# Tiles for the first pair's sums of weights, and the order of units in the head

## The chip, the cores and the metric

The kernel runs on one core of a Trainium2 chip. TensorE (PE) multiplies, ScalarE (ACT) and VectorE (DVE) work elementwise, GpSimd (POOL) takes a few elementwise operations, and SyncE (SP) issues the transfers from HBM. Each engine works through its own instructions in the order in which they stand. The metric is the device time of one execution in microseconds (us).

## What is computed

Two decoder layers work on 512 tokens of width 1024. Each layer is a feed-forward, a token mixer and a second feed-forward. The feed-forwards are what the change touches:

```python
D_MODEL, SEQ, DEPTH, D_FF = 1024, 512, 2, 2816

def swiglu(h, w_up, w_down):
    gate, up = jnp.split(h @ w_up, 2, axis=-1)
    return (jax.nn.silu(gate) * up) @ w_down

for l in range(DEPTH):
    mod = (jnp.einsum('bd,de->be', jax.nn.silu(c), w_ada[l]) + b_ada[l]).reshape(b, 9, d)
    h = modulate(rmsnorm(x, norm_g[l, 0]), mod[:, 0], mod[:, 1])
    x = x + 0.5 * mod[:, 2][:, None] * swiglu(h, w_ffn_in[l, 0], w_ffn_out[l, 0])
    ...          # rmsnorm, modulate, token_mixer, x += mod[:, 5] * y
    h = modulate(rmsnorm(x, norm_g[l, 2]), mod[:, 6], mod[:, 7])
    x = x + 0.5 * mod[:, 8][:, None] * swiglu(h, w_ffn_in[l, 1], w_ffn_out[l, 1])
```

## The kernel before

There are six sub-layers, n = 1 to 6. Numbers 1, 3, 4 and 6 are feed-forwards; 2 and 5 are mixers. In the profiled execution n=3 runs from about 909 to 1268 us, n=4 from there to 1630, and n=6 from about 2158 to the end.

**Products in two parts.** Each float32 operand is split into a rounded high part and the rest. ACT copies the high part (L226 makes `wh` of a weight, L268 `sh`, `ah` of activations) and DVE subtracts it (L230 makes `wl`, L269 `sl`, `al`). Every product is then three matmuls on PE: high by high, low by high, high by low (L274, L276, L278, or the three of L592).

**A feed-forward.** Its 22 blocks of hidden units begin with plain units (two in n=3, 4 and 6, four in n=1), of a gate and an up matrix each. In n=3, 4 and 6 the first three of these four products are the "head" (`head`, L711): 512 tokens in two halves of 256 columns (`HALF`), because the normalised input `h` of the second half comes later. The fourth product ("the fourth unit") follows with all 512 columns. Then come pairs: a pair takes two hidden blocks with seven products in the place of eight (`pair`, `product`, L577 to L648), in the order p = 1, 2, 6, 7, 5, 3, 4, with the next pair's p=1 between 5 and 3. Each of the seven is 24 matmuls of 128x256.

**What a pair needs.** p = 1, 2 and 4 read `h` itself. p = 6, 7, 5 and 3 read four sums of quarters of `h` (`hq`, made in place by `sums`, L559 to L562, and split by `summed` into `sh` and `sl`). On the side of the weights p = 1, 2 and 3 read blocks 11, 21, 22 as they are, and `block` (L233) makes the other four: t1 = w12 - w11 (L246, for p=5), t2 = w22 - t1 (L248, for p=6), w12 = w22 - w12 in place (L250, p=7), w21 = w21 - t2 in place (L253, p=4).

**Rings.** Tiles come from rings of fixed size: raw weights `wraw` 5, `whi` 3, `wlo` 3, the ring of activations `t4k` 10 (sums split, SwiGLU results), and `z` 4. A tile's slot is free once the last reader of its former tile is through. t1 and t2 come from `z` by `z4k`; the four quarters `hq` lie there too and go when `summed` has read them.

**What sets the order.** The program is written sequentially and a scheduler orders the instructions of each engine by their place in the text, the data, the slots of the rings and its own estimate of times. `load` fetches weights in the order of `plan`, two ahead of their use (`AHEAD`), and a pair's sums are made in `load` at p = 6, 7 and 4. The norm of the next half of the tokens (sum of squares L481, the sum over partitions on PE L322, reciprocal root L295 to L307, `h` in L500 to L509) runs on DVE and ACT beside the head.

Of the kernel before, what the change touches and what calls it, by code (L numbers as in the profile page):

```python
# [13 lines left out]
F32 = mybir.dt.float32  # L14
# [6 lines left out]
P = 128  # L21
T = 512
D = 1024
KD = 8
# [10 lines left out]
HALF = (slice(0, 256), slice(256, 512))  # L35
# [38 lines left out]
class Trunk:  # L74
# [44 lines left out]
    def z4k(self, s):  # L119
        t = self.ap_.tile([P, 2 * (T + TAPS - 1)], F32, tag="z", name=self.name(s), bufs=4)  # L120
        return t[:, 0:D]

    def bank(self, tag):
        return self.pp.tile([P, T], F32, tag=tag, name=self.name(tag),
                            bufs={"mm": 4, "s": 3, "o": 1}[tag])
# [76 lines left out]
    def load(self):  # L202
        key = next(self.keys, None)
        if key is None:
            return
        kind = key[0]
        if kind == "up":
            raw, n = self.block(*key[1:]), 1024
        else:
            src, n = self.source(key)  # L210
            raw = self.raw()
            r = raw[:, :n]
            if len(src.shape) == 3:
                r = r.rearrange("p (a b) -> p a b", b=src.shape[2])
            self.nc.sync.dma_start(r, src)
        self.loaded.append((key, *self.halves(key, raw, n)))
# [13 lines left out]
        eng.tensor_tensor(lo[:, :n], raw[:, :n], hi[:, :n].bitcast(F32), op=ALU.subtract)  # L230
        return hi, lo

    def block(self, l, f, j, p):  # L233


        sub = self.nc.vector.tensor_tensor
        if p == 1:
            self.pairs[j] = {}
            for q in (11, 21, 12, 22):
                t = self.raw()  # L240
                self.nc.sync.dma_start(t, self.io["w_up"][l, f, j, (11, 21, 12, 22).index(q)])
                self.pairs[j][q] = t
        b = self.pairs[j]
        if p == 6:
            b["t1"] = self.z4k("t")
            sub(b["t1"], b[12], b[11], op=ALU.subtract)  # L246
            b["t2"] = self.z4k("t")
            sub(b["t2"], b[22], b["t1"], op=ALU.subtract)  # L248
        elif p == 7:
            sub(b[12], b[22], b[12], op=ALU.subtract)  # L250
        elif p == 4:

            sub(b[21], b[21], b["t2"], op=ALU.subtract)  # L253
        return b[{1: 11, 2: 21, 6: "t2", 7: 12, 5: "t1", 3: 22, 4: 21}[p]]
# [326 lines left out]
    def product(self, l, f, j, p, bank, first):  # L581

        nc = self.nc
        w = self.weight("up", l, f, j, p)
        acts = self.operand(p)
        for mi in range(2):
            o = bank[:, mi * 256:mi * 256 + 256]
            for k in range(4):
                c = slice((mi * 4 + k) * P, (mi * 4 + k + 1) * P)
                for x, (a, b) in enumerate(((0, 0), (1, 0), (0, 1))):  # L590

                    nc.tensor.matmul(o, w[a][:, c], acts[k][b], start=first and (mi, k, x) == (0, 0, 0),  # L592
                                     stop=(k, x) == (3, 2), skip_group_check=True)
# [122 lines left out]
    def head(self, take):  # L716

        ws = [take(j) for j in range(3)]
        ps = [self.bank("mm") for _ in ws]
        for k in range(KD):  # L720
            for j in range(3):
                self.mm(ps[j], ws[j], slice(k * P, (k + 1) * P), self.h[k], k == 0, k == KD - 1, HALF[0])
        for j in range(3):
            self.mmk(ps[j], ws[j], self.h, range(KD), 0, KD - 1, HALF[1])
        return ps
# [531 lines left out]
```

## Time and profile before

| | us |
|---|---|
| median of three runs | 2522.96 (2520.47 to 2523.03) |
| the profiled execution | 2520.49 |
| its span | 2518.7 |
| PE busy | 2470.0 (98%) |
| PE weight load busy | 2186.7 (87%) |
| DVE busy | 1924.0 (76%) |
| ACT busy | 1179.6 (47%) |

The span is what the trace covers; 1.8 us lie around it. A row of a timeline gives start, busy time of one and, in brackets, the idle time of the engine before it with what ended it. [...] Matmuls overlap in the pipeline, so the time of a run of them is told by start to start and not by the busy time of one.

### The profile page before, as it was taken

What the parts mean: (1) busy time and instruction counts of PE and PEld (TensorE: products, weight loads), DVE (VectorE), ACT (ScalarE), POOL (GpSimd) and SP (SyncE); (2) the same over time, 40 slices, a digit from 0 to 9 for tenths busy, and PEclk for the clock granted to TensorE, in tenths of its full rate; (3) what the DMA queues carried; (4) which work ended last, traced back from release to release, by engine and by line L of the source; (5) the groups of instructions that cost most, each with busy time, mean ns of one, the idle gap of its engine ahead of it and who ended that gap; (6) DMA issues with size and microseconds to landing.
All of it is one profiled execution on the core that took longest, in us unless ns stands there. A gap on an engine that the chain in (4) does not pass through costs nothing.

```text
span 2518.7 us, 37996 instructions
## 1 busy us (share of the span) xinstructions
PE 2470.0 (98%) x15072; PEld 2186.7 (87%) x15072; DVE 1924.0 (76%) x3344; ACT 1179.6 (47%) x1941; POOL 15.3 (1%) x25
## 2 busy tenths in 40 slices
PE   7999999999999999999989999999999999999999
PEld 6889898888778889898989898898887888898988
DVE  8989876999855478888688796669997654885855
ACT  6535243665653355353455353436665433553523
POOL 0000000000000000000000000000000000000000
PEclk9999999999999999999999999999999999999999
DMA  8565644322223224646325554322222233133332
GB/s 275 185 238 171 231 148 130 95 63 68 78 85 109 94 67 133 234 134 234 126 67 159 209 172 130 101 81 79 64 80 67 82 111 100 59 106 96 111 98 86
DMA packets 97748, 312.21 MB, mean 124 GB/s; under 512 B 10345, under 2 KB 17257, under 8 KB 97570
## 3 DMA queue, kind: packets, MB, share of 16 engines
q1 hardware_dynamic: 97424, 309.65, 38.3%
q8 instruction: 118, 1.93, 0.3%
q14 instruction: 60, 0.49, 0.1%
q10 hardware_dynamic: 146, 0.14, 0.0%
HBM read 307.62 MB, written 6.06 MB: 125 GB/s over the span
## 4 chain that ended last, share of the span: by engine, by line
PE 86%; DVE 9%; ACT 3%; issue 2%; DMA 1%; SPq 0%; DVEq 0%; ACTq 0%
PE mm L592 16%; PE mm L274 14%; PE mm L276 14%; PE mm L278 14%; PE s L592 12%; PE mm L845 3%; PE mm L843 3%; PE mm L841 3%; PE s L904 2%; DVE wl L230 2%; PE o L973 1%; PE s L946 1%; DVE wr L778 1%; ACT wh L226 1%; ACT hh L502 1%
## 5 line engine op out<-in xcount | busy, mean ns | idle before, releaser
L226 ACT ACTIVATE wh<-wr 128x1024 fp32r<-128x1024 f32 (+1 forms) x481 | 485.5, 1011 | 601.2 <-PE mm L278 295.0
L230 DVE TENSOR_TENSOR wl<-wr,wh 128x1024 fp32r<-128x1024 f32 (+1 forms) x476 | 551.6, 1161 | 215.7 <-ACT wh L226 214.5
L276 PE MATMUL mm<-hh,wl 128*128 128x512 f32 (+1 forms) x776 | 281.2, 366 | 5.2 <-DVE wl L230 5.2
L274 PE MATMUL mm<-hh,wh 128*128 128x512 f32 (+1 forms) x776 | 281.1, 365 | 4.8 <-ACT hh L502 2.9
L278 PE MATMUL mm<-al,wh 128*128 128x512 f32 (+1 forms) x752 | 284.8, 379 | 0.0
L276 PE MATMUL mm<-ah,wl 128*128 128x512 f32 (+1 forms) x752 | 283.9, 378 | 0.0
L274 PE MATMUL mm<-ah,wh 128*128 128x512 f32 (+1 forms) x752 | 283.4, 377 | 0.0
L592 PE MATMUL mm<-sh,wh 128*128 128x256 f32 x936 | 268.4, 287 | 12.8 <-ACT wh L226 10.0
L278 PE MATMUL mm<-hl,wh 128*128 128x512 f32 (+1 forms) x776 | 274.9, 365 | 0.7 <-DVE hl L509 0.6
L592 PE MATMUL mm<-sh,wl 128*128 128x256 f32 x936 | 267.6, 286 | 0.9 <-DVE wl L230 0.9
L592 PE MATMUL mm<-sl,wh 128*128 128x256 f32 x936 | 267.3, 286 | 0.0
L518 DVE SCALAR_TENSOR_TENSOR x<-mm,res,x 128x512 f32<-128x512 f32 (+1 forms) x124 | 86.0, 696 | 144.8 <-PE mm L278 144.6
L592 PEld LDWEIGHTS mm<-sh,wh 128*128 128x128 f32 x936 | 181.7, 194 | 14.9 <-ACT wh L226 11.0
L592 PEld LDWEIGHTS mm<-sh,wl 128*128 128x128 f32 x936 | 182.2, 195 | 1.6 <-DVE wl L230 1.2
L592 PEld LDWEIGHTS mm<-sl,wh 128*128 128x128 f32 x936 | 182.2, 195 | 0.0
L843 PE MATMUL mm<-wl,hh 128*128 128x384 f32 x512 | 179.5, 351 | 0.0
L841 PE MATMUL mm<-wh,hh 128*128 128x384 f32 x512 | 179.4, 350 | 0.0
L845 PE MATMUL mm<-wh,hl 128*128 128x384 f32 x512 | 178.8, 349 | 0.0
L592 PE MATMUL s<-hl,wh 128*128 128x256 f32 x624 | 175.2, 281 | 0.0
L592 PE MATMUL s<-hh,wh 128*128 128x256 f32 x624 | 174.8, 280 | 0.0
L592 PE MATMUL s<-hh,wl 128*128 128x256 f32 x624 | 174.0, 279 | 0.5 <-DVE wl L230 0.5
L440 DVE SCALAR_TENSOR_TENSOR ada<-ada,cb 128x1024 f32<-128x1024 f32 x144 | 172.9, 1215 | 1.2 <-DMA ada<-in_w_ada 1.0
(217 smaller groups left out, 5536.8 us busy)
## 6 DMA issues: line engine op xcount, KB each, us to landing
wr<-in_w_up SPq DMA_DIRECT2D x156, 512.0 KB, 3.7
ada<-in_w_ada SPq DMA_DIRECT2D x144, 512.0 KB, 5.5
wr<-in_w_down SPq DMA_DIRECT2D x64, 512.0 KB, 5.3
wr<-in_w_qkv SPq DMA_DIRECT2D x64, 384.0 KB, 3.2
wr<-in_w_gate SPq DMA_DIRECT2D x48, 512.0 KB, 3.6
wr<-in_w_down SPq DMA_DIRECT2D x32, 384.0 KB, 3.2
wr<-in_w_branch SPq DMA_DIRECT2D x24, 512.0 KB, 3.7
wr<-in_w_u SPq DMA_DIRECT2D x16, 512.0 KB, 3.6
```

Of the source, the lines that this page charges most:

```text
L226: nc.scalar.activation(hi[:, :n], raw[:, :n], AF.Copy)
L230: eng.tensor_tensor(lo[:, :n], raw[:, :n], hi[:, :n].bitcast(F32), op=ALU.subtract)
L274: nc.tensor.matmul(ps[:, rng], w[0][:, wcol], ah[:, rng], start=start, stop=False)
L276: nc.tensor.matmul(ps[:, rng], w[1][:, wcol], ah[:, rng], start=False, stop=False)
L278: nc.tensor.matmul(ps[:, rng], w[0][:, wcol], al[:, rng], start=False, stop=stop)
L440: nc.vector.scalar_tensor_tensor(w, w, 1.0, cb, op0=ALU.mult, op1=ALU.mult, accum_out=self.mod[l][:, e:e + 1])
L518: self.nc.vector.scalar_tensor_tensor(self.x[d][:, rng], ps[:, rng], self.res[l][:, 8 * s + d:8 * s + d + 1], self.x[d][:, rng], op0=ALU.m ...
L592: nc.tensor.matmul(o, w[a][:, c], acts[k][b], start=first and (mi, k, x) == (0, 0, 0), stop=(k, x) == (3, 2), skip_group_check=True)
L841: nc.tensor.matmul(o, hi[:, hs], w[0][:, ws], start=k == 0, stop=False)
L843: nc.tensor.matmul(o, hi[:, hs], w[1][:, ws], start=False, stop=False)
L845: nc.tensor.matmul(o, lo[:, hs], w[0][:, ws], start=False, stop=k == KD - 1)
L904: nc.tensor.matmul(ps[:, 0:w], q[r, a, qs], k[r, b, 0:w], start=x == 0, stop=x == 2)
```

## The change

It has two parts. First, `load` hands `block` the place from which t1 and t2 come: for the first pair of each feed-forward (j = 2 in n=1, j = 1 elsewhere) that is the ring `t4k` by a new `t4w`, for all other pairs `z4k` as before. Second, `head` writes the matmuls of the first half of the tokens as units 0 and 1 together over the eight chunks k, then unit 2, where it wrote all three units per chunk. `head` is used by the mixers too.

```diff
+    def t4w(self, s):
+        return self.t4k([P, D], F32, s)
 ...
         if kind == "up":
-            raw, n = self.block(*key[1:]), 1024
+            early = key[3] == (2 if key[1:3] == (0, 0) else 1)
+            raw, n = self.block(*key[1:], self.t4w if early else self.z4k), 1024
 ...
-    def block(self, l, f, j, p):
+    def block(self, l, f, j, p, home):
 ...
         if p == 6:
-            b["t1"] = self.z4k("t")
+            b["t1"] = home("t")
             sub(b["t1"], b[12], b[11], op=ALU.subtract)
-            b["t2"] = self.z4k("t")
+            b["t2"] = home("t")
             sub(b["t2"], b[22], b["t1"], op=ALU.subtract)
 ...
-        for k in range(KD):
-            for j in range(3):
-                self.mm(ps[j], ws[j], slice(k * P, (k + 1) * P), self.h[k], k == 0, k == KD - 1, HALF[0])
+        for js in ((0, 1), (2,)):
+            for k in range(KD):
+                for j in js:
+                    self.mm(ps[j], ws[j], slice(k * P, (k + 1) * P), self.h[k], k == 0, k == KD - 1, HALF[0])
```

Line numbers after the change are 5 higher from `block` on: L246 becomes L251, L230 becomes L235, L269 becomes L274, L509 becomes L514. The rows of SP and of POOL stand in the same order in both kernels. DVE's change in n=3 at three places, and in n=4 and n=6 in the same way. wr_9092, wr_9094, wr_9096 and wr_9098 are blocks 11, 21, 12 and 22 of the first pair; wl_8925 and wl_8931 are the low parts of the head's third unit and of the fourth unit; wl_9101, 9136, 9171, 9201 and 9236 those of p = 1, 2, 6, 7 and 5; sl_9205, 9240 and 9280 the sums of activations of p = 6, 7 and 5.

DVE in n=3, from the end of the first half's `h` to the norm of the second, before:

```order
L518 SCALAR_TENSOR_TENSOR x<-mm_8664,res_113,x 128x256
L509 SCALAR_TENSOR_TENSOR hl_97<-hx_8784,shift_109,hh_96 128x256
L481 TENSOR_TENSOR ssq<-ssq,sq_8814 128x256
L325 TENSOR_SCALAR ts_8848<-s_8843 128x2
L295 TENSOR_SCALAR rs_8850<-ts_8848 128x2
L298 TENSOR_SCALAR nh_8851<-ts_8848 128x2
L296 TENSOR_SCALAR rs_8850<-rs_8850 128x2
L303 SCALAR_TENSOR_TENSOR rt_8852<-rs_8850,nh_8851 128x1 x2
L307 SCALAR_TENSOR_TENSOR rs_8850<-rt_8852,rs_8850 128x1
L230 TENSOR_TENSOR wl_8925<-wr_8922,wh_8924 128x1024
```

and after:

```order
L523 SCALAR_TENSOR_TENSOR x<-mm_8664,res_113,x 128x256
L514 SCALAR_TENSOR_TENSOR hl_97<-hx_8784,shift_109,hh_96 128x256
L251 TENSOR_TENSOR t_9166<-wr_9096,wr_9092 128x1024
L486 TENSOR_TENSOR ssq<-ssq,sq_8814 128x256
L235 TENSOR_TENSOR wl_8925<-wr_8922,wh_8924 128x1024
L330 TENSOR_SCALAR ts_8848<-s_8843 128x2
L300 TENSOR_SCALAR rs_8850<-ts_8848 128x2
L303 TENSOR_SCALAR nh_8851<-ts_8848 128x2
L301 TENSOR_SCALAR rs_8850<-rs_8850 128x2
L308 SCALAR_TENSOR_TENSOR rt_8852<-rs_8850,nh_8851 128x1 x2
```

t1's subtraction (now L251) has come from behind the head to a place ahead of the sum of squares of the second half, and wl_8925 stands ahead of the reciprocal root and no longer inside it.

DVE in n=3, at the end of the second half's `h` (hl_95 and hl_97 are its last two chunks), before:

```order
L509 SCALAR_TENSOR_TENSOR hl_95<-hx_8903,shift_109,hh_94 128x256
L509 SCALAR_TENSOR_TENSOR hl_97<-hx_8908,shift_109,hh_96 128x256
L559 TENSOR_TENSOR hq_8895<-hq_8874,hq_8895 128x1024
L560 TENSOR_TENSOR hq_8874<-hq_8750,hq_8874 128x1024
L230 TENSOR_TENSOR wl_8931<-wr_8928,wh_8930 128x1024
L561 TENSOR_TENSOR hq_8750<-hq_8895,hq_8750 128x1024
```

and after:

```order
L514 SCALAR_TENSOR_TENSOR hl_95<-hx_8903,shift_109,hh_94 128x256
L253 TENSOR_TENSOR t_9168<-wr_9098,t_9166 128x1024
L514 SCALAR_TENSOR_TENSOR hl_97<-hx_8908,shift_109,hh_96 128x256
L564 TENSOR_TENSOR hq_8895<-hq_8874,hq_8895 128x1024
L255 TENSOR_TENSOR wr_9096<-wr_9098,wr_9096 128x1024
L235 TENSOR_TENSOR wl_8931<-wr_8928,wh_8930 128x1024
L565 TENSOR_TENSOR hq_8874<-hq_8750,hq_8874 128x1024
```

t2 (L253) now stands ahead of the last chunk of `h`, and the new w12 (L255) ahead of the low part of the fourth unit, wl_8931; the second of the sums of quarters (L560, now L565) has gone behind it.

DVE in n=3, the first pair's operands, before:

```order
L663 TENSOR_TENSOR sil_9129<-sil_9129,mm_9104 128x512
L269 TENSOR_TENSOR sl_9205<-hq_8750,sh_9204 128x1024
L269 TENSOR_TENSOR sl_9240<-hq_8874,sh_9239 128x1024
L269 TENSOR_TENSOR al_9089<-sil_9129,ah_9088 128x512
L246 TENSOR_TENSOR t_9166<-wr_9096,wr_9092 128x1024
L269 TENSOR_TENSOR sl_9280<-hq_8895,sh_9279 128x1024
L248 TENSOR_TENSOR t_9168<-wr_9098,t_9166 128x1024
L617 TENSOR_TENSOR c_1521_9163<-c_1521_9163,s_9165 128x512
L250 TENSOR_TENSOR wr_9096<-wr_9098,wr_9096 128x1024
L230 TENSOR_TENSOR wl_9171<-t_9168,wh_9170 128x1024
```

and after:

```order
L668 TENSOR_TENSOR sil_9129<-sil_9129,mm_9104 128x512
L235 TENSOR_TENSOR wl_9136<-wr_9094,wh_9135 128x1024
L274 TENSOR_TENSOR al_9089<-sil_9129,ah_9088 128x512
L235 TENSOR_TENSOR wl_9171<-t_9168,wh_9170 128x1024
L274 TENSOR_TENSOR sl_9205<-hq_8750,sh_9204 128x1024
L235 TENSOR_TENSOR wl_9201<-wr_9096,wh_9200 128x1024
L622 TENSOR_TENSOR c_1521_9163<-c_1521_9163,s_9165 128x512
L274 TENSOR_TENSOR sl_9240<-hq_8874,sh_9239 128x1024
L235 TENSOR_TENSOR wl_9236<-t_9166,wh_9235 128x1024
L274 TENSOR_TENSOR sl_9280<-hq_8895,sh_9279 128x1024
```

The three `sl` no longer stand ahead of the sums of weights: for each product its `wl` and its `sl` follow each other, in the order in which PE asks for them. On ACT `wh_9170` (of t2) and `wh_9200` have moved in the same way ahead of the second and third `sh`.

## Rows read from the trace of the kernel before

**Rows 1.** PE's waits by line and releaser: us in total, times, longest us

```profile
PE mm L592 <- ACT wh L226: 10.0, 5, 2.7
PE s L592 <- ACT wh L226: 5.6, 5, 1.3
PE mm L276 <- DVE wl L230: 5.2, 3, 2.0
```

**Rows 2.** PE timeline, first pairs of n=3, 4, 6: start, us, instruction [idle before]

```profile
943.42 0.28 PE L592 MATMUL s<-hl,wh 128*128 128x256 f32 x1
946.31 0.38 PE L592 MATMUL mm<-sh,wh 128*128 128x256 f32 x1 [2.62 <-ACT wh L226]
948.04 0.39 PE L592 MATMUL s<-sh,wh 128*128 128x256 f32 x1 [1.35 <-ACT wh L226]
...
1306.24 0.38 PE L592 MATMUL mm<-sh,wh 128*128 128x256 f32 x1 [2.72 <-ACT wh L226]
...
2194.80 0.58 PE L592 MATMUL mm<-sh,wh 128*128 128x256 f32 x1 [2.62 <-ACT wh L226]
```

**Rows 3.** Chain that ended last, over the span: start, us, piece (first: n=3)

```profile
955.44 8.59 PE mm L592 x72
...
1316.38 8.59 PE mm L592 x72
...
2204.47 8.59 PE mm L592 x72
```

**Rows 4.** Engines by stretch: us, PE, PEld, DVE, ACT, POOL, PEclk, DMA share, GB/s

```profile
948.40:951.70 3.30, 3.30 (x19) 3.30 (x18) 3.30 (x4) 0.55 (x1) 0.00 (x0) 0.51 0.21 27
...
1279.50:1282.80 3.30, 3.30 (x18) 3.30 (x17) 1.97 (x9) 1.08 (x3) 0.00 (x0) 0.51 0.56 159
```

**Rows 5.** DVE timeline, n=3, ahead of the first pair's p=6

```profile
941.62 1.22 DVE L246 TENSOR_TENSOR t<-wr,wr 128x1024 f32<-128x1024 f32 x1
...
943.89 1.22 DVE L248 TENSOR_TENSOR t<-wr,t 128x1024 f32<-128x1024 f32 x1
...
945.63 1.22 DVE L250 TENSOR_TENSOR wr<-wr,wr 128x1024 f32<-128x1024 f32 x1
```

**Rows 6.** ACT timeline, n=3, the same stretch

```profile
945.20 1.06 ACT L226 ACTIVATE wh<-t 128x1024 fp32r<-128x1024 f32 x1 [2.72 <-DVE t L248]
```

**Rows 7.** DVE timeline, n=3, between the halves of the head

```profile
915.63 0.47 DVE L509 SCALAR_TENSOR_TENSOR hl<-hx,shift,hh 128x256 fp32r<-128x256 f32 x1
916.21 0.43 DVE L481 TENSOR_TENSOR ssq<-ssq,sq 128x256 f32<-128x256 f32 x1
917.84 0.16 DVE L325 TENSOR_SCALAR ts<-s 128x2 f32<-128x2 f32 x1 [1.21 <-PE s L322]
...
918.78 1.23 DVE L230 TENSOR_TENSOR wl<-wr,wh 128x1024 fp32r<-128x1024 f32 x1
```

**Rows 8.** PE timeline, n=3, the head's third unit

```profile
920.06 0.39 PE L276 MATMUL mm<-hh,wl 128*128 128x256 f32 x1 [1.57 <-DVE wl L230]
```

**Rows 9.** DVE timeline, n=3, end of the second half's h

```profile
928.40 0.48 DVE L509 SCALAR_TENSOR_TENSOR hl<-hx,shift,hh 128x256 fp32r<-128x256 f32 x1 [0.31 <-ACT hh L502]
...
931.20 1.22 DVE L230 TENSOR_TENSOR wl<-wr,wh 128x1024 fp32r<-128x1024 f32 x1
```

**Rows 10.** PE timeline, n=3, the fourth unit's second matmul and p=1's first

```profile
932.47 0.50 PE L276 MATMUL mm<-hh,wl 128*128 128x512 f32 x1
...
937.94 0.28 PE L592 MATMUL mm<-hh,wh 128*128 128x256 f32 x1
```

**Rows 11.** SP's issues of raw weights w12 and w22, n=3

```profile
910.71 0.33 SPq L241 DMA_DIRECT2D wr<-in_w_up  x1
...
920.03 0.33 SPq L241 DMA_DIRECT2D wr<-in_w_up  x1
```

**Rows 12.** From issue to landing of these two: least, median, most

```profile
DMA to landing us min/median/max: 3.6/3.6/3.6
```

**Rows 13.** DVE's waits by line and releaser: us in total, times, longest us

```profile
DVE t L248 <- DMA wr<-in_w_up: 42.5, 27, 3.8
```

## The prediction

> **What bounds the kernel now.** I read PE's waits first, because PE is busy nearly throughout (the table above): only what takes a wait away from it, or a spell at half clock, can shorten this kernel. In the list of PE's waits [rows 1] the two largest entries have one cause: L592, the pair's matmuls, waits for ACT's high part of a weight, 10.0 us in 5 places (as `mm`) and 5.6 us in 5 (as `s`). The timeline of PE says where [rows 2]: at the first pair of n=3, 4 and 6, where p=6 waits 2.62, 2.72 and 2.62 us. A few matmuls later p=7 waits too, 1.35 us in n=3. Who is late there? ACT's copy `wh<-t` at 945.20 had itself waited 2.72 us for DVE's t2 [rows 6]. And DVE had not been waiting for data: it made t1 at 941.62, an `sl`, t2 at 943.89 and the new w12 at 945.63 [rows 5], one behind the other. Rows of 1024 columns cost DVE 1.14 us from start to start ((943.89 - 941.62)/2), so DVE is late because of its order, and its order is late because t1 and t2 need `z` slots that the quarters hold until `summed` has read them.
>
> [...]
>
> **What the first pair loses in all.** p=2's last matmul starts at 943.42 in n=3, so p=6 was due at 943.54. p=6 and p=7 are 48 matmuls, 48 x 0.119 = 5.73 us, so p=5 was due at 949.27. It starts at 955.44 [rows 3]: 6.2 us lost. In n=4 and n=6 I take p=6's start less its wait less the same 0.15 by which that differs in n=3 (946.31 - 2.62 - 943.54): due at 1303.37 and 2192.03 [rows 2], p=5 due at 1309.10 and 2197.76, started at 1316.38 and 2204.47 [rows 3]: 7.3 and 6.7 lost. Together 20.2 us, of which the p=6 waits are 8.0, and the rest p=7's waits, the half clock and the restarts.
>
> **Does the change take it away?** The cover must be walked through on DVE, in n=3, by the order of after and the durations of before.
>
> *Between the halves of the head.* DVE ends the first half's `h` at about 916.05 [rows 7]. t1 now follows: w12's transfer was issued at 910.71 and took 3.6 [rows 11, 12], so its data are there at 914.3, 1.7 us early, and t1 takes 916.05 to 917.2. The sum of squares, behind it, ends at 917.6 and not at 916.6: one microsecond late. The third unit's `wl` comes next, ahead of the reciprocal root, and ends at 917.6 + 1.2 = 918.8, where before it ended at 918.78 + 1.23 = 920.0; PE waited 1.57 us for it [rows 8]. So PE resumes 1.2 us earlier. The root, the chain on which the second half hangs, loses 1.0 to t1 and wins 1.1: `wl` stood inside it and now stands where DVE had been idle for 1.21 us, waiting for PE's sum [rows 7]. Net about nothing for the second half. Had DVE no such idle time, t1 would cost its 1.14.
>
> *The fourth unit.* t2 goes ahead of the last chunk of `h`. Before, that chunk had 0.31 us of idle time ahead of it and started at 928.40 [rows 9]; now it starts at about 929.2, and PE, which is 1.2 us ahead, has enough matmuls of the earlier chunks left to be through with the head at about 931.5. Ahead of the fourth unit's `wl` stand t2 and the new w12, 2 x 1.14 more, less the second sum of quarters that went behind it (1.14) and the idle 0.31: 0.8 later. It ended at 931.20 + 1.22 = 932.4, just in time for the matmul at 932.47 [rows 10]; now 933.2. PE waits there some 1.5 us where it did not wait, and the net delay against before is 0.8.
>
> *The first pair.* From 933.2 the fourth unit needs 937.94 - 932.47 = 5.5 us [rows 10]: p=1 at 938.7, with its `wl` at 938.9 (five rows of DVE and itself behind the fourth unit's, 4 x 1.14 + 2 x 0.6 for the 512-column ones, an estimate that takes half a row for half the columns). p=1 and p=2 take 5.73: p=6 is due at 944.5. By the row order of after its `wl` is done at about 942.8 and its `sl` at 943.9; p=7 is due at 947.3 with `wl` at 945.1 and `sl` at 946.8; p=5 at 950.2 with `sl` at 949.1. Every one is in time, by 0.5 us at the tightest, so the waits at p=6 and p=7 go, and with them their half clock. p=5 starts at 950.2 instead of 955.4: 5.2 us gained, which is 6.2 removed less 0.9 to 1.0 paid at the fourth unit and p=1.
>
> The same in n=4 and n=6: 7.3 - 0.9 = 6.4 and 6.7 - 0.9 = 5.8. Sum 17.4 us.
>
> *n=1* has no head of this kind and one short wait in its first pair, inside the 5.6 of [rows 1]. Its p=6 sums come earlier, but the first matmul of the next p=7 too, behind a copy that is later. I take 0, bounded by 1.3 of gain (the largest single `s` wait [rows 1]) and 1.5 of loss (the new fourth-unit kind of wait).
>
> **The head's order** is the part with little in it. In n=3, 4 and 6 the third unit already waited behind the two others for its low part (PE's 5.2 us in 3 places at L276 [rows 1]), since the scheduler had put units 0 and 1 first; the new text repeats that. In the mixers no low part was waited for (the three places are the feed-forwards'), so nothing is there to gain, and at most another such wait of 1.57 [rows 8] to lose in each. I take 0.
>
> **What is given back.** (a) The transfers of the second pair are issued as slots come free, and PE will now arrive 5 to 7 us earlier at them. DVE already waits 42.5 us in 27 places for w22 [rows 13], and PE's waits at L592 outside the places named come to about 2.4 us in the whole kernel (10.0 - 8.0 and 5.6 less four p=7 waits of some 1.3 [rows 1, 2]). Bounds: nothing, if the slack holds as in later pairs, and twice 2.4. I take 2.4, the size of what is there. (b) The new wait at the fourth unit is of 1.5 us. Waits of 1.57 in n=3's head left the clock alone; behind that of n=4, the longest of its line with 2.0 [rows 1], 18 matmuls went at 0.51 [rows 4], so (28 - 18) x 0.119 = 1.2 us were lost. Three new waits between the two: I take one spell, 1.2, with bounds of none and three (3.6).
>
> 17.4 - 2.4 - 1.2 = 13.8, so about 14 us. The profiled execution took 2520.49, as the fastest of the runs did, and would come to 2506.5; against the median of 2522.96, 2.5 above it, that is 2509.
>
> [...]
>
> **Rivals.**
> *The gain is half eaten.* Spells behind all three new waits (3.6), the transfers at their bound (4.8) and n=1's loss of 1.5: 17.4 - 9.9 = 7.5, 2515.5. For it: DVE's order is full, and the tightest operand is 0.5 us early. Against it: the pairs further on have the same operands and transfers to wait for, without the head's slack, and cost PE 2.4 us in all. 2512 to 2517.9.
> *The wait only moves.* t2 waits in front of the last chunk of `h`, and w12 in front of the fourth unit's `wl`; if these cost PE what p=6 and p=7 did, 5 us at each of three places, the gain is 17.4 - 15 = 2.4 and the time 2520.5, no change. Each lost microsecond needs DVE to be later by one than the rows say; w22, issued at 920.03 and landing at 923.6 [rows 11, 12], is not what holds it at 928.
> *Slower: t1 at the head of DVE's queue.* If w12 is not there at 916, DVE waits in t1 and the sum of squares, the root and all of the second half's `h` wait behind it. The slack is 1.7 us. To be 5 us slower over three feed-forwards t1 must lose 14 + 5 = 19 us, 6.3 each: landing 11.6 us after issue where it took 3.6. The longest that DVE waited for such a transfer was 3.8 [rows 13]; with the landing that late, 2528.
> [...]
> *The change does not do what it says.* Tiles of `t4k` could be held by something else; the order of after shows t1 and t2 early, so only the head's half can be empty, and it is priced at 0.
>
> **How the numbers follow.** Forecast (10 to 19 gained): 0.62. Half eaten (5 to 10): 0.20. Wait moves (within 5): 0.12. Slower: 0.06. A measurement of this kernel can tell some 0.2%, 5 us, from no change. Faster by over 0.2%: 0.62 + 0.20 = 0.82; same 0.12; slower 0.06. The range reaches from 2502 (all of 20.2 removed and nothing given back) to 2518, the end of the half-eaten case, which leaves out 0.18.
>
> **What would show it.** Right: in n=3 no wait at p=6 and p=7; PE's p=5 some 11.5 us behind p=1; a new wait of 1 to 2 us at the fourth unit's second matmul, released by DVE's `wl`; the head's third unit waiting 0.4 us or less. Wrong: waits at p=6 or p=7 of over half a microsecond; a clock near 0.5 behind the fourth unit in more than one of the three; L592 waiting longer in the second pairs; DVE idle at t1 for a transfer. The prediction is wrong if `sl` or `wl` of p=6 ends behind 944.5 in the time of n=3, or if the new wait at the fourth unit is 4 us and not 1.5.

## The result, and the profile after

| | before | after |
|---|---|---|
| median, us | 2522.96 (2520.47 to 2523.07) | 2505.52 (2503.83 to 2507.23) |
| ratio | | 0.9935, 95% interval 0.9923 to 0.9947 |
| span of the profiled execution | 2518.7 | 2502.0 |

The change takes 17.4 us away; 14 were forecast, 2509 within 2502 to 2518. Two later measurements of the same kernel beside the one before gave 0.9936 and 0.9933. Of 41 executions of the kernel before that were measured beside the experiments, the five shortest (2520.54 to 2520.96) have a mean granted clock of 0.995 or 0.996 of full speed and the five longest (2525.24 to 2526.33) of 0.993; the profiled one (2520.49, 0.995) is as short as the shortest.

PE's waits in the kernel after (us in total, times, longest), the lines that answer to [rows 1]:

```profile
PE mm L279 <- ACT wh L231: 3.9, 5, 0.9
...
PE mm L597 <- ACT wh L231: 2.7, 3, 1.0
...
PE mm L281 <- DVE wl L235: 2.4, 2, 1.2
...
PE s L597 <- ACT wh L231: 1.2, 2, 0.8
```

The 10.0 and 5.6 us of waiting for `wh` in the pairs have become 2.7 and 1.2. The head's third unit, which had waited 1.57, 2.03 and 1.56 us for DVE's `wl` (the 5.2 of L276), now waits 0.56, 0.94 and 0.56 us for ACT's `wh` (L279); the other two waits in that line, of 0.93 each, are in the mixers, and the kernel before has them too. New is the wait of the fourth unit for DVE's `wl` (L281), 1.21 us in n=3 and in n=6. PE's timeline in n=3 shows this wait and then the first pair without one: the fourth unit's second matmul, p=2's last, p=6's first, p=7's first, p=5's first.

```profile
933.26 0.50 PE L281 MATMUL mm<-hh,wl 128*128 128x512 f32 x1 [1.21 <-DVE wl L235]
...
944.63 0.28 PE L597 MATMUL s<-hl,wh 128*128 128x256 f32 x1
944.74 0.29 PE L597 MATMUL mm<-sh,wh 128*128 128x256 f32 x1
...
947.62 0.28 PE L597 MATMUL s<-sh,wh 128*128 128x256 f32 x1
...
950.49 0.28 PE L597 MATMUL mm<-sh,wh 128*128 128x256 f32 x1
```

These answer to [rows 2, 10]: p=6 follows p=2 at 0.11 us, where it stood 2.62 us, and p=7 and p=5 follow at 2.88 and 2.87. In the chain that ended last the pieces of [rows 3] now read, for n=3 and n=6:

```profile
950.66 8.59 PE mm L597 x72
...
2187.79 8.59 PE mm L597 x72
```

And in the stretches of [rows 4] the half clock is gone (columns as there; the third is longer, and held 26 matmuls at 0.51 before):

```profile
948.40:951.70 3.30, 3.30 (x30) 3.30 (x30) 3.30 (x4) 2.86 (x4) 0.00 (x0) 1.00 0.00 0
1279.50:1282.80 3.30, 3.30 (x29) 3.25 (x28) 3.05 (x8) 3.30 (x10) 0.00 (x0) 1.00 0.00 0
1306.80:1313.50 6.70, 6.70 (x59) 6.70 (x58) 5.95 (x6) 3.21 (x5) 0.00 (x0) 1.00 0.65 221
```

DVE in n=3, the rows that answer to [rows 7, 9]: t1 behind the last chunk of the first half, and t2 and w12 around the last of the second.

```profile
916.36 1.22 DVE L251 TENSOR_TENSOR t<-wr,wr 128x1024 f32<-128x1024 f32 x1
917.50 0.41 DVE L486 TENSOR_TENSOR ssq<-ssq,sq 128x256 f32<-128x256 f32 x1
917.83 1.22 DVE L235 TENSOR_TENSOR wl<-wr,wh 128x1024 fp32r<-128x1024 f32 x1
919.12 0.16 DVE L330 TENSOR_SCALAR ts<-s 128x2 f32<-128x2 f32 x1
...
928.19 1.22 DVE L253 TENSOR_TENSOR t<-wr,t 128x1024 f32<-128x1024 f32 x1
929.32 0.48 DVE L514 SCALAR_TENSOR_TENSOR hl<-hx,shift,hh 128x256 fp32r<-128x256 f32 x1
929.72 1.22 DVE L564 TENSOR_TENSOR hq<-hq,hq 128x1024 f32<-128x1024 f32 x1
930.86 1.22 DVE L255 TENSOR_TENSOR wr<-wr,wr 128x1024 f32<-128x1024 f32 x1
931.99 1.22 DVE L235 TENSOR_TENSOR wl<-wr,wh 128x1024 fp32r<-128x1024 f32 x1
```

Stage by stage, with the start of DVE's last product of each feed-forward (L638, now L643) as the mark of its end: n=1 ends 0.38 us later than before, n=3 then 4.1 earlier, n=4 11.2, n=6 16.7. The gain at a first pair alone is read from the start of p=5 (1316.22 and 1304.55 on PE's timeline in n=4) against what the kernel brought along from the feed-forward ahead. Two more executions of the changed kernel were profiled beside the experiments; by the same marks all three stand like this (us gained against the profile before, a minus for us lost):

| execution, span | n=1 | first pair of n=3 | rest of n=3 | first pair of n=4 | rest of n=4 | first pair of n=6 |
|---|---|---|---|---|---|---|
| the one shown, 2502.0 | -0.4 | 5.2 | -0.7 | 7.5 | -0.4 | 5.4 |
| second, 2504.4 | -0.1 | 5.1 | -2.0 | 6.6 | -0.7 | 5.4 |
| third, 2505.6 | -0.5 | 5.2 | -3.3 | 6.5 | -0.6 | 5.6 |

So the first pairs gain 17.1 to 18.1 us in each, and what is lost again behind them in n=3 and n=4 goes from 1.1 to 4.0. The larger gain in n=4 goes with the clock. The head of n=4 waits 0.93 to 0.94 us in all three; a little later the second execution has a stretch at 0.50 (1276.0 to 1279.4) and the third one at 0.51 (1276.4 to 1279.8), and the one shown has none. First the one shown, then the second:

```profile
1276.00:1279.40 3.40, 3.33 (x29) 3.13 (x28) 3.18 (x9) 2.66 (x7) 0.00 (x0) 1.00 0.03 12
...
1276.00:1279.40 3.40, 3.40 (x18) 3.40 (x18) 2.03 (x11) 0.62 (x2) 0.00 (x0) 0.50 0.42 146
```

### The profile page after: what moved, and what is told of

The parts are those of the page before. It is cut to its first block, busy times and chain, and to the rows that moved or that the text cites. A ratio compares the mean times of both kernels' runs of the same rounds, so it can differ in the third digit from the quotient of the medians.

```text
span 2502.0 us, 38006 instructions
## 1 busy us (share of the span) xinstructions
PE 2463.8 (98%) x15072; PEld 2179.1 (87%) x15072; DVE 1923.3 (77%) x3344; ACT 1179.7 (47%) x1941; POOL 15.6 (1%) x25
## 4 chain that ended last, share of the span: by engine, by line
PE 84%; DVE 9%; ACT 2%; DMA 2%; issue 2%; SPq 0%; DVEq 0%; ACTq 0%
PE mm L597 14%; PE mm L279 14%; PE mm L281 14%; PE mm L283 14%; PE s L597 11%; PE mm L852 3%; PE mm L850 3%; PE mm L848 3%; PE s L911 2%; DVE wl L235 2%; DMA wr<-in_w_up 2%; PE o L980 1%; PE s L953 1%; DVE wr L785 1%; ACT wh L231 1%
## 5 line engine op out<-in xcount | busy, mean ns | idle before, releaser
L235 DVE TENSOR_TENSOR wl<-wr,wh 128x1024 fp32r<-128x1024 f32 (+1 forms) x476 | 552.2, 1163 | 204.7 <-ACT wh L231 203.3
L279 PE MATMUL mm<-hh,wh 128*128 128x512 f32 (+1 forms) x776 | 281.4, 366 | 7.0 <-ACT wh L231 3.9
L279 PE MATMUL mm<-ah,wh 128*128 128x512 f32 (+1 forms) x752 | 283.5, 377 | 0.0
L281 PE MATMUL mm<-ah,wl 128*128 128x512 f32 (+1 forms) x752 | 283.4, 378 | 0.0
L281 PE MATMUL mm<-hh,wl 128*128 128x512 f32 (+1 forms) x776 | 280.8, 365 | 2.6 <-DVE wl L235 2.4
L279 PEld LDWEIGHTS mm<-hh,wh 128*128 128x128 f32 x776 | 145.9, 188 | 34.7 <-ACT wh L231 5.4
```

The costliest lines, as they stand in the source:

```text
L279: nc.tensor.matmul(ps[:, rng], w[0][:, wcol], ah[:, rng], start=start, stop=False)
L281: nc.tensor.matmul(ps[:, rng], w[1][:, wcol], ah[:, rng], start=False, stop=False)
```

## The experiments

**1. The tiles alone.**

```diff
-        for js in ((0, 1), (2,)):
-            for k in range(KD):
-                for j in js:
 ...
+        for k in range(KD):
+            for j in range(3):
 ...
```

> The change with the old head: t1 and t2 of each first pair from the ring of activations, the head's first half written with three units per chunk as before. In the written order this differs from the changed kernel only by nine matmuls of PE in the head of the mixer n=2. Theory (the tiles are the whole gain): 2505.5, within 1.5 of the changed kernel. Rival (the head's order has a share): 2508 or more, with the head's third unit in n=3 waiting longer than the 0.56 us it waits in the changed kernel.

Measured: 2506.24, ratio to before 0.9931 (0.9916 to 0.9946). The tiles are the whole gain. This kernel also showed the step that hands something back. PE at p=2 of a later pair in n=3, and DVE ahead of it:

```profile
1001.08 0.39 PE L597 MATMUL s<-hh,wl 128*128 128x256 f32 x1 [0.77 <-DVE wl L235]
```

```profile
998.66 1.23 DVE L253 TENSOR_TENSOR t<-wr,t 128x1024 f32<-128x1024 f32 x1 [2.82 <-DMA wr<-in_w_up]
999.81 1.22 DVE L235 TENSOR_TENSOR wl<-wr,wh 128x1024 fp32r<-128x1024 f32 x1
```

DVE stood 2.82 us in t2 for w22's transfer, and p=2's `wl`, behind it in DVE's order, came 0.77 us late. By the marks of the table its profiled execution lost 2.6 us in the rest of n=3, in which this wait and one of 0.69 us like it at 1106 lie; the three executions of the changed kernel, with the same order there, lost 0.7, 2.0 and 3.3. So this price varies from execution to execution.

**2. t1 alone early.**

```diff
-            b["t2"] = home("t")
+            b["t2"] = self.z4k("t")
```

> The changed kernel with only t1 in the ring of activations; t2 takes a slot of z again. Theory (the first pair hangs on the slot of t2, which comes free only behind the first split of a sum): t2's subtraction stays behind three splits, p=6 keeps a wait for its high part of about 1.4 us and gets one of about 3 for its low part, the whole stall keeps nearly its length: 2519 to 2523, p=5 of n=3 starting at 954 to 956. Rival (DVE is late by so many rows, and two rows of 1.14 less in front of p=6 give 2.3 us back at each of three pairs): 2514 to 2517.

Measured: 2516.08, 0.9972 (0.9961 to 0.9984), the number of the rival. PE's timeline in n=3:

```profile
945.22 0.38 PE L597 MATMUL mm<-sh,wh 128*128 128x256 f32 x1 [0.41 <-ACT wh L231]
946.17 0.39 PE L597 MATMUL s<-sh,wh 128*128 128x256 f32 x1 [0.56 <-ACT wh L231]
948.07 0.58 PE L597 MATMUL mm<-sh,wl 128*128 128x256 f32 x1 [1.52 <-DVE wl L235]
```

The places are those of the theory: t2 is still behind the splits, p=6 waits for its high and then longer for its low part (0.41 and 1.52 us, where 1.4 and 3 were expected), and p=5 of n=3 starts at 955.08, 0.2 earlier than before. What I left out is the clock. The stall is now three shorter waits; in n=3 the clock still fell to 0.51 (947.8 to 951.2), but behind the waits of n=4 it stayed up:

```profile
1304.00:1311.00 7.00, 4.46 (x33) 3.87 (x33) 7.00 (x7) 3.47 (x4) 0.00 (x0) 1.00 0.14 25
```

In its profiled execution n=4's first pair gained 4.4 us by the marks of the table, and n=6's and n=3's 1.0 and 0.6. So t1 alone is worth about a third of the change, most of it at the one pair where the clock stayed up, and t2's slot the other two thirds.

**3. The wait filled with matmuls** (the kernel before):

```diff
 ...
+        if p == 2 and j == 1:
+            o = self.bank("o")
+            for q in range(22):
+                nc.tensor.matmul(o[:, 0:256], w[1][:, 0:P], acts[q % 4][0],
+                                 start=q == 0, stop=q == 21, skip_group_check=True)
```

> The kernel before, with 22 more matmuls of 128x256 on PE between p=2 and p=6 of the first pair in n=3, 4 and 6 (low part of p=2's weight by high parts of h, into a bank that nobody reads; the result is untouched). They take 22 x 0.117 = 2.6 us and lie in the wait of 2.6 to 2.7, so the wait itself stays. Theory (part of the loss is the half clock behind the wait): the granted clock behind p=6 is 1.0 and p=5 starts 1.0 to 1.5 us earlier in n=3 and 2 to 2.5 in n=4 and n=6: 2517 to 2519. Rival (the loss is all waiting, or p=7's wait of 1.35 brings the spell by itself): 2521 to 2523.5, clock 0.51 there as before.

Measured: 2516.88, 0.9977 (0.9967 to 0.9986): the kernel becomes faster by work that nobody reads. PE in n=3, p=7's and p=5's first matmuls, and the engines' row of the stretch behind p=7's wait:

```profile
949.01 0.39 PE L592 MATMUL s<-sh,wh 128*128 128x256 f32 x1 [1.34 <-ACT wh L226]
...
954.74 0.28 PE L592 MATMUL mm<-sh,wh 128*128 128x256 f32 x1
```

```profile
949.70:953.00 3.30, 3.30 (x30) 3.30 (x29) 3.30 (x4) 1.03 (x3) 0.00 (x0) 1.00 0.25 47
```

p=7's wait of 1.34 us is still there, and the clock is 1.00 behind it, so here that wait does not bring the spell by itself. From p=7 to p=5 it takes 5.73 us where it took 7.23; in n=4 and n=6 5.74 and 5.73 where it took 8.25 and 7.77. That is 6.1 us of half clock at the three pairs, three tenths of the 20.2 that the prediction counted there. The waits at p=6 and p=7 were 8.0 and 3.9 before. Part of the 6.1 was lost elsewhere in this profiled execution, and by the clock again: behind the third unit's wait of 1.56 us in n=3 and in n=6 PE went at 0.51 (919.6 to 923.0, 2165.6 to 2169.0), where the profile before has 1.00 behind 1.57 and 1.56.

**4. t1 twice** (the changed kernel):

```diff
+            if home == self.t4w and (l, f) != (0, 0):
+                sub(b["t1"], b[12], b[11], op=ALU.subtract)
```

> The changed kernel with t1 of the first pair computed twice in n=3, 4 and 6; in the written order the second subtraction stands in the reciprocal root of the second half's norm. It prices DVE's time at that place, which a late transfer of w12 would take. Theory (the root is the chain on which the second half of h hangs, and the idle time that hid t1 is used up): the fourth unit's second matmul in n=3 starts 0.9 to 1.2 us later, 2508 to 2509.5. Rival (there is still cover): within 1 us of the changed kernel, 2504.5 to 2506.5.

Measured: 2510.3, 4.1 above the tiles alone beside it (0.9947, 0.9932 to 0.9962). PE in n=3 waits for the second half's `h`, and the fourth unit comes later:

```profile
925.34 0.39 PE L281 MATMUL mm<-hh,wh 128*128 128x256 f32 x1 [1.11 <-ACT hh L509]
935.61 0.50 PE L283 MATMUL mm<-hh,wl 128*128 128x512 f32 x1 [1.22 <-DVE wl L235]
```

In the run with the tiles alone the second of these stood at 934.22; 0.39 of the difference was there when the head began, so 1.0 us is paid for 1.14 us of DVE, as the theory said. By the marks of the table the three first pairs come 1.0, 1.4 and 1.2 us later than with the tiles alone. t1's place is free once and not twice: the idle time that hid it is used up.

**5. t2 and w12 on GpSimd** (with n=1's first pair as before, here and in the edited kernels that follow):

```diff
+        eng = self.nc.gpsimd.tensor_tensor if home == self.t4w else sub
 ...
-            sub(b["t2"], b[22], b["t1"], op=ALU.subtract)
+            eng(b["t2"], b[22], b["t1"], op=ALU.subtract)
 ...
-            sub(b[12], b[22], b[12], op=ALU.subtract)
+            eng(b[12], b[22], b[12], op=ALU.subtract)
```

> The changed kernel with two edits: in n=3, 4 and 6 GpSimd makes t2 and the new w12 of the first pair in the place of DVE, and n=1's first pair takes t1 and t2 from z as before. DVE's row order then has the last chunk of h, the first two sums of quarters and the fourth unit's low part behind one another. Theory (the fourth unit waits for DVE's time and nothing else): its wl ends 0.8 us earlier in n=3, 4 and 6, the wait of 1.21 falls to 0.4 or less, and n=1 wins 0.4 back: 2502 to 2503.5. Rival (GpSimd's row takes twice as long, 2.4 us, and slows DVE's rows beside it, or p=6 now waits for t2): 2505 to 2508.

Measured: 2513.83, 0.9963 (0.995 to 0.9975), 7.6 above the changed kernel beside it. The rival's reason, at a higher price than it gave. GpSimd, DVE and PE in n=3:

```profile
922.97 2.36 POOL L254 TENSOR_TENSOR t<-wr,t 128x1024 f32<-128x1024 f32 x1 [11.87 <-DVE hx L506]
...
923.17 2.44 DVE L515 SCALAR_TENSOR_TENSOR hl<-hx,shift,hh 128x256 fp32r<-128x256 f32 x1
925.54 0.47 DVE L506 SCALAR_TENSOR_TENSOR hx<-x,amp,s 128x256 f32<-128x256 f32 x1
925.93 2.20 DVE L515 SCALAR_TENSOR_TENSOR hl<-hx,shift,hh 128x256 fp32r<-128x256 f32 x1
...
925.67 0.58 PE L284 MATMUL mm<-hl,wh 128*128 128x256 f32 x1 [1.62 <-DVE hl L515]
```

A row of DVE that takes 0.47 us takes 2.44: it ends 0.3 us after GpSimd's. DVE gave away two rows of 1.14 and paid two stops of nearly 2 us in the chain of `h`. The half clock is part of the price too: from 925.8 to 932.6, behind the wait of 1.62, PE started 29 matmuls at 0.51, where the changed kernel started 52 at 1.00.

**6. All other t1 on GpSimd as well.**

```diff
-            sub(b["t1"], b[12], b[11], op=ALU.subtract)
+            (sub if home == self.t4w else self.nc.gpsimd.tensor_tensor)(b["t1"], b[12], b[11], op=ALU.subtract)
```

> The same as the run with t2 and w12 on GpSimd, and in all later pairs (and in n=1) GpSimd makes t1. Theory (what is given back further on is DVE standing in t1 for the transfer of w12, with p=2's low part behind it): DVE's waits for transfers at t1 vanish, PE's waits at L597 for wl fall below 1 us and the run-to-run spread narrows; 1 to 2 us below the run with t2 and w12 alone. Rival (the pairs are bound by the transfer of w22, at t2, or the longer t1 delays t2): same time or up to 3 us more.

The changed kernel ran beside these two:

> The changed kernel once more, so that the two runs with GpSimd and it stand beside each other on one chip: 2505.5 within 1.5.

Measured: 2506.24 (0.9936, 0.9923 to 0.9948) for that, and here 2537.78, 1.0063 (1.0049 to 1.0076): slower, beyond what the rival gave. DVE's waits at t2 and PE's for low parts (us in total, times, longest):

```profile
DVE t L254 <- DMA wr<-in_w_up: 76.3, 31, 3.2
...
PE s L598 <- DVE wl L235: 9.1, 15, 0.7
```

With nothing to stop it at t1, DVE runs to t2 and stands there for w22, 76.3 us, where it stood 45.5 in experiment 5 and 42.5 in the kernel before [rows 13]. That fits the rival, by which w22's transfer paces the later pairs; it is not shown apart. How much of the 24 us over experiment 5 is that and how much is DVE stopped by 36 more rows of GpSimd, this run does not tell.

**7. The fourth unit's low part in two halves.**

```diff
-        eng.tensor_tensor(lo[:, :n], raw[:, :n], hi[:, :n].bitcast(F32), op=ALU.subtract)
+        parts = 2 if kind == "in" and key[3:] == (1, 1) and key[1:3] != (0, 0) else 1
+        for i in range(parts):
+            c = slice(i * n // parts, (i + 1) * n // parts)
+            eng.tensor_tensor(lo[:, c], raw[:, c], hi[:, c].bitcast(F32), op=ALU.subtract)
```

> The changed kernel with n=1's first pair as before and, in n=3, 4 and 6, the low part of the fourth unit's weight made in two halves of 512 columns. Theory (the fourth unit waits for DVE's low part alone, and its first four chunks need only the first half): the wait of 1.21 us becomes 0.6 to 0.7, and n=1 wins back 0.4: 2503 to 2504.5. Rival (p=1 or p=6 takes the 0.57 up, since DVE is no earlier there): 2505 to 2506.5.

Measured: 2505.57, 0.9928 (0.9914 to 0.9942). PE in n=3, the fourth unit's second matmul and p=1's second:

```profile
932.53 0.50 PE L284 MATMUL mm<-hh,wl 128*128 128x512 f32 x1 [0.68 <-DVE wl L238]
...
939.07 0.38 PE L600 MATMUL mm<-hh,wl 128*128 128x256 f32 x1 [0.68 <-DVE wl L238]
```

The wait falls to 0.68 as forecast, and p=1 takes the gain up, since DVE is through with its own rows no earlier. The rival's account holds.

**8. p=7's weight over w11.**

```diff
+            if home == self.t4w:
+                sub(b[11], b["t2"], b[11], op=ALU.subtract)
+                return b[11]
             sub(b[12], b[22], b[12], op=ALU.subtract)
```

> The changed kernel with n=1's first pair as before and, in n=3, 4 and 6, p=7's weight made as t2 - w11 over w11 (the same sum) and not as w22 - w12 over w12. It cannot stand ahead of p=1's low part any more, and in the written order t2 moves forward to the end of the reciprocal root, ahead of all of the second half's h. There its data are not there yet: w22 was issued at about 919 to 920 in n=3 and takes 3.6. Theory (DVE stands still for a late transfer and what is queued behind it pays one for one): DVE waits 1 us or more for the transfer in t2, the second half's first hx starts about 2 us later than the 921.92 of the changed kernel, the fourth unit's wl, for which two rows less stand ahead, ends 0.9 later: 2507 to 2509.5. Rival (the second half's h has slack, and two rows less ahead of the fourth unit count): 2502 to 2504.5.

Measured: 2504.15, 0.9924 (0.9908 to 0.994), the rival's number, and my theory's premise was wrong. SP's issue of w22, t2 on DVE, the second half's first `hx`, and PE at the fourth unit and p=7, in n=3:

```profile
917.39 0.33 SPq L246 DMA_DIRECT2D wr<-in_w_up  x1
...
921.07 1.23 DVE L253 TENSOR_TENSOR t<-wr,t 128x1024 f32<-128x1024 f32 x1
922.21 1.26 DVE L508 SCALAR_TENSOR_TENSOR hx<-x,amp,s 128x256 f32<-128x256 f32 x3
...
932.94 0.51 PE L284 MATMUL mm<-hh,wl 128*128 128x512 f32 x1 [0.59 <-DVE wl L235]
...
947.78 0.39 PE L600 MATMUL s<-sl,wh 128*128 128x256 f32 x1 [0.48 <-DVE sl L277]
```

w12's slot is free after t1 now, so w22 goes out at 917.39 and no longer at 919.08, and lands (3.6 us) when DVE comes to t2. t2 slips into the time in which DVE waits for PE anyway, and the second half's `h` begins 0.3 later and not 2. The intended test of a transfer at the head of DVE's queue was therefore not made; the 1.14 us of experiment 4 stand for it.

**9. Both edits, and two repeats.** This is experiments 7 and 8 together.

> The run with p=7's weight made over w11, and the fourth unit's low part in two halves as well. Written order in n=3: t2 ahead of the second half's h, two sums of quarters, the two halves of the fourth unit's low part, and p=6's and p=7's sums of activations one behind the other. Theory (what is left at the fourth unit, 0.59 us, is DVE's low part, and p=7's 0.48 us its late sum): both waits fall below 0.2 us in n=3 and n=6, 1.5 to 2.5 us below the changed kernel's time of the same call. Rival (p=1 or p=7's weight takes it up, as p=1 took up 0.68 us when the halves alone were tried): within 1 us of the run with w11 alone.

> The run with p=7's weight over w11 once more, beside the changed kernel on one chip. Theory (a row less of DVE ahead of the fourth unit, and w22 on its way 1.5 us earlier into the slot that w12 leaves): 1 to 2.5 us below the changed kernel. Rival (the difference seen, 2504.15 against 2505.5 to 2506.2, is spread): within 0.7 us of it.

> The changed kernel a third time, to stand beside the two runs with p=7's weight made over w11 on one chip: 2505 to 2507.

Measured beside one another: both 2501.2 (0.9911, 0.9897 to 0.9925), w11 alone 2504.73 (0.9927, 0.9914 to 0.9939), the changed kernel 2506.63 (0.9933, 0.9919 to 0.9946). w11 alone is 1.9 below the changed kernel, with intervals that overlap widely. Both together are 5.4 below it, more than forecast. The intervals of the two ratios still overlap a little (0.9919 to 0.9925), but each of the four executions with both edits is shorter than any of the changed kernel or of w11 alone. All of PE's waits in n=3 from 900 to 960 us are then:

```profile
PE mm L285 <- ACT hh L513: 0.6, 1, 0.6
PE mm L285 <- ACT wh L231: 0.6, 1, 0.6
PE mm L289 <- DVE hl L520: 0.3, 1, 0.3
PE s L342 <- DVE rs L318: 0.2, 1, 0.2
```

Nothing is left at the fourth unit or in the first pair. The order has changed as well: with the halves the scheduler puts p=7's sum of activations ahead of its `wl`, and PE does not wait there any more. By the marks of the table the profiled executions of both edits and of the changed kernel beside them stand 5.5 us apart: 3.4 at the three first pairs, 0.6 in n=1, and 1.5 in the rest of n=3 and n=4, which is no more than executions of the changed kernel differ by there. In n=4 the stretch at 0.51 in the head, which this execution of the changed kernel has, is missing with both edits.

## Why the prediction was right, step by step

- **What bounds it.** Right, and the right size: 20.2 us were counted at the three first pairs and of them 11.9 are waits at p=6 and p=7 and 6.1 half clock (experiment 3); the other 2.2 were not measured apart.
- **Between the halves of the head.** Right to 0.1 us. Everything in n=3 stands 0.35 later than in the profile before, when the first half's `h` begins; with that, t1, the sum of squares and the third unit's `wl` end where the prediction put them (917.5, 917.9, 919.05). The reciprocal root begins at 919.12 and not at 917.84, and without `wl` inside it the second half's first `hx` still starts at 921.92 (921.73 before), so the second half loses nothing, as forecast. The wait of the third unit was to be 0.4 or less; it is 0.56 in n=3 and n=6 and 0.94 in n=4, and for ACT's `wh`, which was not looked at.
- **The fourth unit.** Right: wait of 1.21 us where 1.5 were forecast, the second matmul at 933.26 where 933.2 + 0.35 was forecast, the release by DVE's `wl`. In n=4 it is 0.83, and PE names ACT's `wh` of p=1, whose first matmul the scheduler had placed ahead.
- **The first pair.** p=6, p=7 and p=5 were due at 944.9, 947.7 and 950.5 with the offset and stand at 944.74, 947.62 and 950.49. In n=6 5.4 us were gained where 5.8 were forecast.
- **n=4** was forecast with 6.4. The profiled execution gained 7.5, the two others 6.6 and 6.5. The spell at half clock in its head, priced at 1.2 in (b) as a danger, was also there in the kernel before, 18 matmuls at 0.51 [rows 4]. Where it stays, with 18 and 19 matmuls at 0.50 and 0.51 in the two others, the term was right; where it does not come, the term was 1.1 too small. I listed the spell and did not credit its going.
- **n=1** was set to 0. The profiled execution ends it 0.4 later: the wait of p=7 for its high part (1.33) is replaced by one of 0.59 for its `sl` and, in the second pair, of 0.8 for a `wh`. That this is a price of the change is not shown. The kernels of experiments 5, 7, 8 and 9 that have n=1's first pair as before end n=1 at 341.4 to 342.4, and the three executions of the changed kernel at 341.7 to 342.0.
- **What is given back.** For the transfers 2.4 were forecast, with bounds of 0 and 4.8. The three executions show 1.1, 2.8 and 4.0, by the step named (p=2's `wl` behind t2's wait), so 2.4 is a fair middle of a price that varies. The new half-clock spell of 1.2 behind the fourth unit came in none of the three: the clock is 1.00 there in n=3, n=4 and n=6. The bound of three spells is not borne out either, behind waits of 0.83 and 1.21 us there. The 0.119 us of a matmul, 8.59/72 of [rows 3], held: from p=6 to p=5 in n=3 the kernel after takes 5.75 us where 48 x 0.119 = 5.73 were forecast, and at 1.00 it starts 30 and 29 matmuls in the two stretches of 3.3 us of [rows 4], where 28 were counted.
- **The sum and the median.** 13.8 were forecast between two profiled executions; the three came to 16.7, 14.3 and 13.1. The 2506.5 that this gave stands among their times, 2503.83, 2506.24 and 2507.42. To it the prediction added 2.5, by which the median of the kernel before lies above its profiled execution. The changed kernel's medians (2505.52, 2506.24, 2506.63) lie around 2506 and show nothing of that 2.5, and this is most of what 2509 was too high by. The granted clocks above suggest that the longer executions of the kernel before hold more half clock, which the change takes away as well; no run here shows it.
- **The head's order.** Right: nothing to measure. Without it PE's order differs only at some matmuls of n=2's head, and the time is the same (2506.24 in experiment 1).
- **The rivals.** Half eaten: the place is right, and up to 4.0 of its bound of 4.8 for the transfers were paid, but no spell behind the fourth unit and nothing clear in n=1. The wait that only moves: it moves, for 1.2 us and not 5. Slower by t1 at the head of DVE's queue: DVE's time there is indeed priced at nearly one for one (experiment 4), but w12 was there in time.

## What to carry to other kernels

When an engine is late with an operand though it waits for no data, ask which ring of tiles holds its instruction back: two tiles moved to a ring with free slots gave 0.65% here. Put the wait and the half-speed stretch behind it on one bill, since three tenths of this one were the clock, and a shorter or filled wait can save that part alone. And when work is moved forward in a queue, price it by the idle time it fills there: the first 1.14 us of DVE were free, the next cost 1.0.

## What the runs showed of the hardware

In the rows read here DVE's `hl` ends only when GpSimd's row beside it is through, and `hx` keeps its usual time. In experiment 5 `hl` took 2.44 and 2.20 us, where in n=3 after the change it takes 0.47 to 0.49 with no row of GpSimd beside it, and the `hx` between the two took 0.47. Both kernels have the effect already, where GpSimd makes the low part of the head's second unit; here it is in n=3 after the change, and in the last row `hx` with no row of GpSimd beside it:

```profile
908.30 1.27 DVE L505 SCALAR_TENSOR_TENSOR hx<-x,amp,s 128x256 f32<-128x256 f32 x3 [0.35 <-PE s L336]
908.62 2.42 POOL L235 TENSOR_TENSOR wl<-wr,wh 128x1024 fp32r<-128x1024 f32 x1 [527.66 <-ACT wh L231]
...
909.48 1.83 DVE L514 SCALAR_TENSOR_TENSOR hl<-hx,shift,hh 128x256 fp32r<-128x256 f32 x1
911.24 0.47 DVE L505 SCALAR_TENSOR_TENSOR hx<-x,amp,s 128x256 f32<-128x256 f32 x1
...
921.92 1.26 DVE L505 SCALAR_TENSOR_TENSOR hx<-x,amp,s 128x256 f32<-128x256 f32 x3 [0.74 <-PE s L336]
```

Three `hx`, the last two beside GpSimd's row, take 1.27 us, and three without such a row 1.26; `hl` takes 1.83 and ends 0.27 behind GpSimd's row. Why the one row is held up and the other is not, no run here shows.

DVE's 3344 and ACT's 1941 instructions start, line by line, in the order in which they are written, in both profiles. In experiment 1 p=2's `wl`, written behind t2, started behind t2's wait of 2.82 us.

Whether a wait of PE is followed by half clock is not settled by its length alone: 1.34 us behind filled work left the clock at 1.00 (experiment 3), 1.35 behind the wait of 2.62 left it at 0.51 [rows 2, 4]. Nor is it the same each time in one place: behind the third unit's wait in n=4 (0.93 to 0.94 us) two of three executions of the changed kernel had a stretch at 0.50 or 0.51 and one had none, and behind 1.56 to 1.57 us in n=3 the profile before shows 1.00 and that of experiment 3 shows 0.51. So a price of the half clock that is read from one execution, as in (b) of the prediction, is uncertain by a whole spell.
